# Transposing SwiGLU results by DMA in 16-bit halves instead of on TensorE

## The chip, the core and the metric

The kernel runs on one core of one Trainium2 chip. Its time is the device time of one execution in microseconds, here the median of three runs. The engines of the core are TensorE (PE in the profile; PEld is its weight load), VectorE (DVE), ScalarE (ACT), GpSimd (POOL) and SyncE (SP). SP and GpSimd issue the loads of the weights; sixteen DMA engines carry them out.

## What is computed

Two layers of a hybrid decoder on one sequence of 512 tokens with 1024 features, all in float32:

```python
for l in range(DEPTH):                      # DEPTH = 2
    x = x + 0.5 * swiglu(rms_norm(x, ffn1_norm[l]), ffn1_wg[l], ffn1_wu[l], ffn1_wd[l])
    h = rms_norm(x, mix_norm[l])
    z = h @ w_in[l]                         # q, k, v and three inputs of a short convolution
    ...                                     # sliding-window attention (128), gated convolution
    x = x + concat([attn_out, conv_out]) @ w_out[l]
    x = x + 0.5 * swiglu(rms_norm(x, ffn2_norm[l]), ffn2_wg[l], ffn2_wu[l], ffn2_wd[l])
return rms_norm(x, final_norm)

def swiglu(h, w_gate, w_up, w_down):        # 1024 -> 2816 -> 1024
    return (silu(h @ w_gate) * (h @ w_up)) @ w_down
```

So there are four SwiGLUs, which make up most of the work, and the change touches only these. The 2816 inner features are 22 blocks of 128, taken as 11 pairs of blocks.

## The kernel before

Every float32 product is made of three products of rounded parts: an operand is split into a high part (a cast on ScalarE, L213) and a low part (the difference, on VectorE, L214), and high x high, high x low and low x high are summed in PSUM. This holds for weights (`raw` to `wh` and `wl`, three buffers each) and for activations.

**Groups of seven.** The large products are done as 2 x 2 blocks with seven block products in place of eight. `Seven` (L567) makes the seven forms of the activation side: `b11`, `b21`, `t2`, `t3`, `t1`, `t4`, `b22`, each split into parts in 4 KB buffers (pool `xf`, 14 of them, function `form`). On the weight side the sums of blocks are made by accumulating DMAs on GpSimd's queue (L208, L279) and by additions on VectorE (L249). `CHAINS` gives the order of the seven steps. A step is two weight groups (h = 0 and 1) of twelve matmuls each.

**Stages.** Each SwiGLU is a list of stages. `p` is a plain pair, `w` a pair of inner blocks by seven steps (`winograd2`, L988), `u` the same in another form (`winograd`), `d` a plain down projection of one or two pairs, `s` a down projection of four pairs by seven steps (`share`, L817), and `e` the last one of the program (`Finale.last`). The lists are

```python
FIRST = (("p",0),("p",1),("d",(0,)),("w",2),("d",(1,)),("w",4),("w",6),("w",8),("u",10),("s",2),("d",(10,)),("s",6))
INNER = (("p",0),("d",(0,)),("w",1),("w",3),("w",5),("w",7),("w",9),("s",1),("s",5),("d",(9,10)))
LAST = INNER[:-2] + (("e", 5),)
```

The first SwiGLU uses `FIRST`, the second and third `INNER`, the fourth `LAST`. A stage `s` or `e` takes its activations from `raws`: two pairs make the four blocks of one group of seven. So in each SwiGLU four pairs feed groups of seven (`blocks`), sixteen in all. In the two `INNER` ones pair 9 goes into the plain down projection at the end (with the plain pair that is left over), and in `LAST` pair 9 is handled by `few`.

**The turn.** `winograd2` leaves its results `ups[0..3]` with tokens on the partitions (128 tokens x 512 features each). The down projection needs features on the partitions. `turn(c)` (L1045 on) transposes four 128 x 128 blocks on TensorE into PSUM (L1050), and ScalarE copies the 128 x 512 result to `raws` (L1057; L1054 for `few`), or `split` makes its parts (for pair 9 of `INNER`). The four turns of a pair are kept in `pending` and taken out by `flush`: one each after steps 0 and 1 and two after step 2 of the next stage (`turns`), or in a later `d` or `s` stage.

**Order.** The program is written in the order of the work; a planner gives every engine its own queue, in which instructions stand in the order of the program as far as their inputs and buffers are free at the planned time. `tc.issue_after(ins)` holds what is written in its block behind one given instruction of the same engine. Each queue then runs strictly in order. Weights are loaded four units ahead (`LOAD_AHEAD`) and split two groups ahead (`SPLIT_AHEAD`); SP issues a load (L196) when one of eight `raw` buffers is free.

**Other buffers.** `g2` has 14 buffers of 2 KB per partition (gates, results, evictions, and the eight partial results of `Apart` in the stages `s` of all but the first SwiGLU), `g8` four of 8 KB (`raws` and the scaled input of the norm).

Of the kernel before, what the change touches and what calls it, by code (L numbers as in the profile page):

```python
# [8 lines left out]
F32 = mybir.dt.float32  # L9
F32R = mybir.dt.float32r  # L10
BF16 = mybir.dt.bfloat16
I32 = mybir.dt.int32
AF = mybir.ActivationFunctionType
ALU = mybir.AluOpType

P = 128
D = 1024
S = 512
# [53 lines left out]
def trunk_kernel(  # L72
# [55 lines left out]
    def f32(ap):  # L128
        return ap.bitcast(F32)


    zero = const.tile([P, S], BF16, name="zero")
    nc.vector.memset(zero, 0.0)
# [76 lines left out]
            state["raw"] += 1  # L210

    def split(hi, lo, raw, eng=nc.vector):
        nc.scalar.copy(hi, raw)  # L213
        eng.tensor_sub(lo, raw, f32(hi))  # L214

    def split_far(hi, lo, raw):

# [4 lines left out]
    def need_split(g):  # L222
        while state["split"] <= min(g, len(order) - 1):
# [330 lines left out]
    class Seven:  # L554
# [8 lines left out]
        def make(self, *names):  # L563
            for what in names:
                if what in self.forms:
                    continue
                b11, b12, b21, b22 = (  # L567
                    self.full[j][:, :, t * H : (t + 1) * H] for j in range(2) for t in range(2)
                )
# [319 lines left out]
    def ffn(norm, stages, after=None, late=None):  # L889
# [102 lines left out]
        def winograd2(b, between=None):  # L992
# [47 lines left out]
                if between:  # L1040
                    between(step)
            if b in blocks:
                raws[b] = g8(f"raw_a_{name}", F32, (P, KC // 2, S))
            if b in few:
                raws[b] = [form(f"raw_a{n}_{name}", F32, (P, 2, S)) for n in range(2)]  # L1045

            def turn(c, tag="sc"):
# [5 lines left out]
                if b in few:  # L1053
                    nc.scalar.copy(raws[b][c // 2][:, c % 2, :], tp)  # L1054
                    return
                if b in raws:
                    nc.scalar.copy(raws[b][:, c, :], tp)  # L1057
# [5 lines left out]

            pending.extend(lambda *tag, c=c: turn(c, *tag) for c in range(NT))

        def shared(b):
            return Seven([raws[b], raws[b + 2]], room_form, f"s_{norm.i}_{b}")

        def turns(step):

            if step < 2:
                flush()
            if step == 2:
                flush(2, "mm")

        sevens = [b for what, b in stages if what == "s"]
        blocks = [b + j for what, b in stages if what in "se" for j in (0, 2)]
        few = [b + 4 for what, b in stages if what == "e"]
        raws = {}
        pending = []  # L1080

# [7 lines left out]
        for i, (what, b) in enumerate(stages):  # L1089
# [10 lines left out]
            if what == "s" and end:  # L1100
                ends = [
                    Seven(full, None, f"e_{n}")
                    for n, full in enumerate(([raws[b + 4], raws[b + 6]], raws[b + 8]))
                ]

                def between(step):
# [3 lines left out]
                        if step == at:  # L1110
                            ends[n].make(operand)

                share(ops, 0.5, between, apart)
            elif what == "e":
                end.last(ends)
                return
            elif what == "s" and b == sevens[0]:
# [1 line left out]
                share(  # L1119
                    ops,  # L1120
                    0.5,
                    ahead(then, {3: ("b11",), 4: ("b21",), 5: ("t2",), 6: ("t3",)}),
                    apart,
                )
            elif what == "s" and i + 1 == len(stages):
# [464 lines left out]
```

## Time and profile before

| | |
|---|---|
| median of three runs | 1678.69 us (1678.51 to 1679.63) |
| the profiled execution | 1678.83 us |
| its span, first to last instruction | 1677.0 us |
| granted TensorE clock, mean | 0.999 |
| TensorE matmul, busy | 1668.1 us (99%) |
| VectorE, busy | 1388.3 us (83%) |
| ScalarE, busy | 979.6 us (58%) |
| moved by DMA | 285.15 MB, mean 170 GB/s |

Times are of one profiled execution. A row of a group gives line, engine, operation, output and inputs by their names in the program, shapes and count, then the busy time of the group in us and the mean of one in ns, then idle time of the engine before them and what ended it. A row of a timeline gives start and length in us, both from the start of the span. Matmuls overlap, so that the distance from one start to the next, and not the length, is what one costs. A row of stretches gives the busy time of each engine with its number of instructions, the granted clock, the mean busy share of the sixteen DMA engines, and what they moved in GB/s.

### The profile page before, as it was taken

To read this page: it belongs to the slowest core of one execution; us is meant where nothing else is said; L and a number is where in the kernel's file an instruction comes from. 1 tells how busy PE (TensorE), PEld (TensorE's weight loads), DVE (VectorE), ACT (ScalarE), POOL (GpSimd) and SP (SyncE) were. 2 spreads that over 40 slices of the span, in tenths; PEclk is the share of its full clock that TensorE was granted. 3 is DMA by queue.
4 is the path that set the end of the run, shared out by engine and by line. 5 is a ranking of instruction groups with operands and counts; after the bars stand their busy time and mean duration, and the time that the engine had idled before them with its cause. 6 is when DMAs were issued, how large, how long until landed. Compare 5 with 4: busy or idle time off the path is not lost.

```text
span 1677.0 us, 22346 instructions
## 1 busy us (share of the span) xinstructions
PE 1668.1 (99%) x8396; PEld 1414.0 (84%) x8396; DVE 1388.3 (83%) x1824; ACT 979.6 (58%) x1361; POOL 211.2 (13%) x188
## 2 busy tenths in 40 slices
PE   9999999999999999999999999999999999999998
PEld 7888889988898888888888888888888988888886
DVE  7987679988899976799798677997788998667997
ACT  6445565466566655575465555654565766556655
POOL 0011111001211111111011111110012111111121
PEclk9999999999999999999999999999999999999999
DMA  8467777731497777778567777785125967777892
GB/s 252 99 177 189 188 195 186 188 98 51 113 228 175 177 187 185 183 197 204 173 139 179 187 187 188 189 209 167 51 64 130 233 140 194 185 187 179 224 252 74
DMA packets 192545, 285.15 MB, mean 170 GB/s; under 512 B 9068, under 2 KB 77748, under 8 KB 192436
## 3 DMA queue, kind: packets, MB, share of 16 engines
q1 hardware_dynamic: 151844, 201.26, 38.1%
q0 software_dynamic: 39872, 81.80, 28.6%
q8 instruction: 66, 1.08, 0.3%
q10 hardware_dynamic: 720, 0.66, 0.1%
q14 instruction: 43, 0.35, 0.1%
HBM read 262.71 MB, written 2.10 MB: 158 GB/s over the span
## 4 chain that ended last, share of the span: by engine, by line
PE 96%; issue 1%; DMA 1%; DVE 1%; ACT 0%; POOL 0%; SPq 0%; POOLq 0%; DVEq 0%; ACTq 0%
PE x L813 25%; PE y L813 12%; PE acc L308 8%; PE acc L309 8%; PE acc L311 7%; PE x_s L813 6%; PE w L813 6%; PE y_s L813 3%; PE x_s L798 3%; PE at L1050 2%; PE x_m L798 2%; PE w_s L813 2%; PE y_s L798 1%; PE x_e L813 1%; PE y_m L798 1%; PE acc L693 1%
## 5 line engine op out<-in xcount | busy, mean ns | idle before, releaser
L213 ACT CAST wh<-raw 128x1024 fp32r<-128x1024 f32 (+1 forms) x491 | 513.0, 1045 | 535.8 <-PE x L813 129.1
L214 DVE TENSOR_TENSOR wl<-raw,wh 128x1024 fp32r<-128x1024 f32 (+1 forms) x491 | 598.3, 1221 | 202.8 <-ACT wh L213 201.2
L308 PE MATMUL acc<-xh,wh 128*128 128x512 f32 x424 | 165.8, 392 | 0.0
L309 PE MATMUL acc<-xl,wh 128*128 128x512 f32 x424 | 165.5, 390 | 0.0
L311 PE MATMUL acc<-xh,wl 128*128 128x512 f32 x416 | 162.3, 390 | 0.0
L208 POOL DMA_DIRECT2D raw<-in_ffn_wu_dram x39 | 48.9, 1254 | 419.7 <-DMA raw<-in_ffn_wu_dram 340.2
L309 PEld LDWEIGHTS acc<-xl,wh 128*128 128x128 f32 x424 | 79.7, 188 | 15.9 <-DVE xl L489 0.2
L308 PEld LDWEIGHTS acc<-xh,wh 128*128 128x128 f32 x424 | 79.8, 188 | 15.6
L311 PEld LDWEIGHTS acc<-xh,wl 128*128 128x128 f32 x416 | 78.1, 188 | 16.4
L208 POOL DMA_DIRECT2D raw<-in_ffn_wg_dram x39 | 48.0, 1255 | 221.1 <-DMA raw<-in_ffn_wu_dram 84.1
L208 POOL DMA_DIRECT2D raw<-in_ffn_wd_dram x34 | 41.0, 1207 | 259.4 <-DMA raw<-in_ffn_wd_dram 112.0
L249 DVE TENSOR_TENSOR raw<-raw,raw 128x1024 f32<-128x1024 f32 x56 | 68.0, 1219 | 2.4 <-DMA raw<-in_ffn_wu_dram 1.7
L813 PE MATMUL w<-wh,fb21h 128*128 128x512 f32 x152 | 60.7, 399 | 0.0
L813 PE MATMUL x<-wh,ft2h 128*128 128x512 f32 x152 | 60.6, 398 | 0.0
L813 PE MATMUL y<-wh,ft3h 128*128 128x512 f32 x152 | 60.4, 398 | 0.0
L813 PE MATMUL w<-wl,fb21h 128*128 128x512 f32 x152 | 59.4, 391 | 0.0
L813 PE MATMUL x<-wl,ft2h 128*128 128x512 f32 x152 | 59.3, 390 | 0.0
L813 PE MATMUL y<-wh,ft3l 128*128 128x512 f32 x152 | 59.2, 390 | 0.0
L813 PE MATMUL y<-wl,ft3h 128*128 128x512 f32 x152 | 59.2, 390 | 0.0
L813 PE MATMUL w<-wh,fb21l 128*128 128x512 f32 x152 | 59.2, 389 | 0.0
L813 PE MATMUL x<-wl,fb11h 128*128 128x512 f32 x152 | 59.2, 389 | 0.0
L813 PE MATMUL x<-wh,ft1l 128*128 128x512 f32 x152 | 59.1, 389 | 0.0
(602 smaller groups left out, 4586.4 us busy)
## 6 DMA issues: line engine op xcount, KB each, us to landing
raw<-in_ffn_wu_dram SPq DMA_DIRECT2D x126, 512.0 KB, 4.4
raw<-in_ffn_wd_dram SPq DMA_DIRECT2D x105, 512.0 KB, 5.7
raw<-in_ffn_wg_dram SPq DMA_DIRECT2D x86, 512.0 KB, 4.7
raw<-in_ffn_wu_dram POOLq DMA_DIRECT2D x39, 512.0 KB, 8.1
raw<-in_ffn_wg_dram POOLq DMA_DIRECT2D x39, 512.0 KB, 6.2
raw<-in_w_in_dram SPq DMA_DIRECT2D x36, 512.0 KB, 3.6
raw<-in_ffn_wd_dram POOLq DMA_DIRECT2D x34, 512.0 KB, 9.0
raw<-raw POOLq DMA_DIRECT2D x21, 512.0 KB, 8.3
```

The costliest lines, as they stand in the source:

```text
L208: nc.gpsimd.dma_start(out=r, in_=rows_of(*more), accum_op=ALU.add)
L213: nc.scalar.copy(hi, raw)
L214: eng.tensor_sub(lo, raw, f32(hi))
L249: nc.vector.tensor_add(a11, a11, s1)
L308: nc.tensor.matmul(acc, hi[:, k, :], rhs[k][0], start=k == first, stop=False)
L309: nc.tensor.matmul(acc, hi[:, k, :], rhs[k][1], start=False, stop=False)
L311: nc.tensor.matmul(acc, lo[:, k, :], rhs[k][0], start=False, stop=k == last)
L693: nc.tensor.matmul(opening[n], (lo if part == "w" else hi)[:, k, :], xl if part == "x" else xh, start=n not in begun, stop=k == KC - 1 and ...
L798: nc.tensor.matmul(accs[c // 2][:, c % 2, :], w[:, k, cols], x_[:, 2 * h + k, :], start=start and c % 2 == 0 and h + k + i == 0, stop=h + ...
L813: nc.tensor.matmul(accs[u], x_[:, 2 * h + k, tok], w[:, k, :], start=start and h + k + i == 0, stop=h + k == 2 and i == 2, skip_group_chec ...
L1050: nc.tensor.transpose(tp[:, t * P : (t + 1) * P], ups[t][:, c * P : (c + 1) * P], ident)
```

## The change

The turns on TensorE go away for the sixteen pairs that feed groups of seven and for pair 9 of the two `INNER` SwiGLUs. The four turns of `few` in `LAST` stay. In their place each result of 128 x 512 float32 words is looked at as 1024 halves of 16 bits. ScalarE copies it so that all the low halves lie together and all the high halves lie together (`lay_apart`); SP issues DMA transposes of 16-bit elements from one SBUF tile to another; and ScalarE puts the transposed halves together into words again (`join`).

For a pair of a group of seven (`Crossing`) two of the four results are laid apart and sent after step 0 of the next stage and two after step 1, one DMA of 256 KB each. Two of the four columns are joined after step 5 and two after step 6; for the last of the four pairs all four are joined after step 3 of the stage `s` (`joined`). For pair 9 (`Tail`) the same goes on inside the first stage `s`: laid and sent after steps 1 and 2, with two DMAs of 128 KB for each result, joined after steps 5 and 6, and split in the second stage `s`. The joins stand behind the last weight cast written before them. `Seven` takes its blocks through a function, since they are not there yet when it is made.

```diff
+    def words(ap):
+        return ap.bitcast(U16).rearrange("p (n two) -> p two n", two=2)
+
+    def lay_apart(src, name):
+        halves = g2(f"halves_{name}", U16, (P, 2, S))
+        nc.scalar.copy(halves, words(src))
+        return halves
...
     def split(hi, lo, raw, eng=nc.vector):
-        nc.scalar.copy(hi, raw)
+        cast = nc.scalar.copy(hi, raw)
         eng.tensor_sub(lo, raw, f32(hi))
+        return cast
...
-                split(hi, lo, raw)
+                state["cast"] = split(hi, lo, raw).ins
...
             if b in blocks:
-                raws[b] = g8(f"raw_a_{name}", F32, (P, KC // 2, S))
+                crossing.append(Crossing(b, name, ups))
+                return
+            if b in tails:
+                crossing.append(Tail(b, name, ups))
+                return
...
-                if b in raws:
-                    nc.scalar.copy(raws[b][:, c, :], tp)
-                    return
...
+        class Crossing:
...
+            def step(self):
+                n = self.steps
+                self.steps += 1
+                if n == 0:
+                    self.to = g8(f"turned_{self.name}", U16, (P, 2, NT, S))
+                for t in {0: (0, 1), 1: (2, 3)}.get(n, ()):
+                    halves = lay_apart(self.ups[t], f"{self.name}_{t}")
+                    nc.sync.dma_start_transpose(
+                        self.to.rearrange("p a c s -> p (a c) s")[:, :, t * P : (t + 1) * P],
+                        halves.rearrange("p a n -> p (a n)"),
+                    )
+                if n in (5, 6) and self.b != max(blocks):
+                    self.join(*((0, 1), (2, 3))[n - 5])
+                    return n == 6
+                return False
+
+            def join(self, *cs):
+                if self.b not in raws:
+                    raws[self.b] = g8(f"raw_a_{self.name}", F32, (P, KC // 2, S))
+                with tc.issue_after(state["cast"]):
+                    for c in cs:
+                        nc.scalar.copy(words(raws[self.b][:, c, :]), self.to[:, :, c, :])
+
+        class Tail:
...
+            def during(self, n):
+                if n == 1:
+                    self.to = [form(f"turned{h}_{self.name}", U16, (P, NT, S)) for h in range(2)]
+                for t in {1: (0, 1), 2: (2, 3)}.get(n, ()):
+                    halves = lay_apart(self.ups[t], f"{self.name}_{t}")
+                    for h in range(2):
+                        nc.sync.dma_start_transpose(
+                            self.to[h][:, :, t * P : (t + 1) * P], halves[:, h, :]
+                        )
+                if n == 5:
+                    self.whole = g8(f"raw_a_{self.name}", F32, (P, 2, 2, S))
+                if n > 4:
+                    whole = self.whole[:, n - 5].rearrange("p c s -> p (c s)")
+                    with tc.issue_after(state["cast"]):
+                        for h in range(2):
+                            nc.scalar.copy(
+                                words(whole)[:, h, :],
+                                self.to[h][:, 2 * (n - 5) : 2 * (n - 4), :].rearrange("p c s -> p (c s)"),
+                            )
+
+            def parts(self, j):
+                hi, lo = acts[self.b + j] = [form(f"a{n}_{self.name}_{j}", shape=(P, 2, S)) for n in "hl"]
+                split(hi, lo, self.whole[:, j])
...
+        def joined(between):
+            def step(n):
+                if n == 3:
+                    crossing.pop(0).join(0, 1, 2, 3)
+                if crossing and isinstance(crossing[-1], Tail):
+                    crossing[-1].during(n)
+                between(n)
+            return step
...
         def turns(step):
...
+            crossing[:] = [c for c in crossing if not c.step()]
...
             elif what == "s":
                 def between(step):
-                    if 2 <= step < 6:
-                        flush(1, "aux")
+                    if step in (2, 4):
+                        crossing[0].parts(step // 2 - 1)
```

More of the change, by code (lines that the diff above doesn't have):

```diff
@@ L11 @@
 BF16 = mybir.dt.bfloat16
+U16 = mybir.dt.uint16
 I32 = mybir.dt.int32
@@ L566, in make @@
                     continue
+                full = self.full() if callable(self.full) else self.full
                 b11, b12, b21, b22 = (
-                    self.full[j][:, :, t * H : (t + 1) * H] for j in range(2) for t in range(2)
+                    full[j][:, :, t * H : (t + 1) * H] for j in range(2) for t in range(2)
                 )
@@ L1064, in winograd2, with __init__ @@
             pending.extend(lambda *tag, c=c: turn(c, *tag) for c in range(NT))
-        def shared(b):
-            return Seven([raws[b], raws[b + 2]], room_form, f"s_{norm.i}_{b}")
+        class Crossing:
+            def __init__(self, b, name, ups):
+                self.b, self.name, self.ups = b, name, ups
+                self.steps = 0
+                self.to = None
+            def step(self):
[19 more added lines that the diff above has]
+                        nc.scalar.copy(words(raws[self.b][:, c, :]), self.to[:, :, c, :])
@@ new lines, in ffn, with __init__, step @@
+        class Tail:
+            def __init__(self, b, name, ups):
+                self.b, self.name, self.ups = b, name, ups
+            def step(self):
+                return False
+            def during(self, n):
[20 more added lines that the diff above has]
+                split(hi, lo, self.whole[:, j])
@@ L1074, in turns @@
                 flush(2, "mm")
+            crossing[:] = [c for c in crossing if not c.step()]
+        crossing = []
         sevens = [b for what, b in stages if what == "s"]
@@ L1078, in ffn @@
         few = [b + 4 for what, b in stages if what == "e"]
+        tails = [b[0] for what, b in stages if what == "d" and len(b) == 2]
         raws = {}
@@ L1102, in ffn @@
                     Seven(full, None, f"e_{n}")
-                    for n, full in enumerate(([raws[b + 4], raws[b + 6]], raws[b + 8]))
+                    for n, full in enumerate((lambda b=b: [raws[b + 4], raws[b + 6]], raws[b + 8]))
                 ]
@@ L1111, in between @@
                             ends[n].make(operand)
-                share(ops, 0.5, between, apart)
+                share(ops, 0.5, joined(between), apart)
             elif what == "e":
@@ L1121, in ffn @@
                     0.5,
-                    ahead(then, {3: ("b11",), 4: ("b21",), 5: ("t2",), 6: ("t3",)}),
+                    joined(ahead(then, {3: ("b11",), 4: ("b21",), 5: ("t2",), 6: ("t3",)})),
                     apart,
```

1 line of the change is left out of this document (added).

## The prediction

> **What bounds the kernel now.** I read the busy shares first, then the chain that ended last, then the groups of ScalarE, then the stages one by one. The page's busy shares and its chain:
>
> ```profile
> span 1677.0 us, 22346 instructions
> PE 1668.1 (99%) x8396; PEld 1414.0 (84%) x8396; DVE 1388.3 (83%) x1824; ACT 979.6 (58%) x1361; POOL 211.2 (13%) x188
> ...
> PE 96%; issue 1%; DMA 1%; DVE 1%; ACT 0%; POOL 0%; SPq 0%; POOLq 0%; DVEq 0%; ACTq 0%
> PE x L813 25%; PE y L813 12%; PE acc L308 8%; PE acc L309 8%; PE acc L311 7%; PE x_s L813 6%; PE w L813 6%; PE y_s L813 3%; PE x_s L798 3%; PE at L1050 2%; PE x_m L798 2%; PE w_s L813 2%; PE y_s L798 1%; PE x_e L813 1%; PE y_m L798 1%; PE acc L693 1%
> ```
>
> TensorE is the bound: 96% of the chain is its work, and 2% is line 1050, the transposes that the change takes away. The sum is made against this profiled execution: 1678.83 us, of which the span is 1677.0 and 1.8 lies around it; the median of the three runs, 1678.69, is 0.14 lower, so nothing has to be converted. A difference of 0.2% (3.4 us) is about what a measurement of this kernel can tell from none.
>
> **What is removed from TensorE.** The groups of ScalarE count the turns, since each turn is four transposes and one reading of the result:
>
> ```profile
> L213 ACT CAST wh<-raw 128x1024 fp32r<-128x1024 f32 (+1 forms) x491 | 513.0, 1045 | 535.8 <-PE x L813 129.1 <-issue 93.4 <-PE y L813 84.2
> L1057 ACT COPY raw_a<-at 128x512 f32<-128x512 f32 x64 | 35.8, 586 | 3.1 <-PE at L1050 3.0
> ...
> L1003 ACT COPY p<-x 128x512 f32<-128x512 f32 x38 | 22.2, 585 | 12.0 <-PE x L813 12.0
> ...
> L213 ACT CAST ah<-at 128x512 fp32r<-128x512 f32 x8 | 4.6, 580 | 0.0
> ...
> L1054 ACT COPY raw_a<-at 128x512 f32<-128x512 f32 x4 | 2.1, 586 | 0.0
> ```
>
> 64 turns feed the sixteen pairs of the groups of seven, 8 the two inner last pairs, 4 the last pair of the final SwiGLU. The first 72 go; the 4 of line 1054 stay. What one turn costs the chain is read where it cuts into a row of matmuls (TensorE's timeline; start, duration):
>
> ```profile
> 919.20 0.39 PE L813 MATMUL x<-wh,fb11l 128*128 128x512 f32 x1
> 919.43 0.39 PE L813 MATMUL x<-wl,fb11h 128*128 128x512 f32 x1
> 919.66 0.38 PE L1050 MATMUL at<-ident,u 128*128 128x128 f32 x2
> 919.88 0.38 PE L1050 MATMUL at<-ident,p 128*128 128x128 f32 x2
> 920.01 0.48 PE L813 MATMUL w<-wh,fb21h 128*128 128x512 f32 x1
> 920.33 0.40 PE L813 MATMUL w<-wh,fb21l 128*128 128x512 f32 x1
> 920.56 0.40 PE L813 MATMUL w<-wl,fb21h 128*128 128x512 f32 x1
> ```
>
> A matmul follows the one before by 0.227 us. Without the turn the two matmuls after it would start at 919.66 and 919.89; the second starts at 920.33, so this turn costs 0.44 us, not the 4 x 0.27 that the durations suggest (they overlap). Over a whole pair's stage, from the chain in order of time (two steps at its start, the same place one stage later, and steps between):
>
> ```profile
> 948.86 10.88 PE x L813 x48
> ...
> 960.18 5.50 PE w L813 x24
> ...
> 966.12 5.46 PE x L813 x24
> ...
> 972.45 5.46 PE y L813 x24
> ...
> 988.79 10.88 PE x L813 x48
> ```
>
> The stage is 988.79 - 948.86 = 39.93 us with four turns, and seven steps of 10.88 / 2 = 5.44 would be 38.1: 1.85, or 0.46 a turn, the slower matmuls behind it included. I take that: 72 x 0.46 = 33.1 us. (The page's 2% of 1677 is 33.5 for 76 turns, 0.44 each, 31.7 for 72.)
>
> **What is added to ScalarE.** Per pair, four copies that lay the halves apart and four that join them go in, each of 1024 halves per partition; four copies of 0.586 go out. No row shows a 16-bit copy. The lower end is 0.586 (512 words, as if the halves went two at a time), the upper twice the 128x1024 cast, 2.09; I take the cast's 1.045, which has the same number of elements. Per pair +8 x 1.045 - 4 x 0.586 = +6.0 us, 96 us over sixteen pairs; per tail +8 x 1.045 + 2 x 1.045 - 4 x 0.580 = +8.1, 16 over two. ScalarE goes from 980 to some 1092 of 1646 us. Whether that is hidden is decided by stage. A pair's stage, the last pair's (with the operands for the next group), an inner first group of seven, and the second:
>
> ```profile
> 659.60:699.70 40.10, 40.10 (x187) 33.28 (x186) 27.95 (x29) 22.08 (x29) 5.40 (x5) 1.00 0.74 183
> 699.70:739.70 40.00, 40.00 (x186) 33.22 (x185) 36.61 (x37) 27.71 (x35) 3.76 (x4) 1.00 0.73 184
> 739.70:777.80 38.10, 38.10 (x170) 31.56 (x169) 37.08 (x37) 25.91 (x30) 6.44 (x6) 1.00 0.87 216
> 777.80:820.00 42.20, 42.20 (x207) 35.26 (x206) 33.83 (x40) 18.58 (x21) 4.20 (x4) 1.00 0.75 192
> ```
>
> (The columns are length, then busy TensorE, weight loads, VectorE, ScalarE, GpSimd, then clock, DMA share, GB/s.) An ordinary pair's stage comes to 22.1 + 6.0 = 28.1 of 38.1 us: it fits. Within it the first step has two casts, two evictions and two lays, 2 x 1.045 + 2 x 0.585 + 2 x 1.045 = 5.35 of a step's 5.44: full, but not over, and the casts have slack:
>
> ```profile
> 940.51 1.05 ACT L213 CAST wh<-raw 128x1024 fp32r<-128x1024 f32 x1 [1.19 <-PE x L813]
> 943.23 1.05 ACT L213 CAST wh<-raw 128x1024 fp32r<-128x1024 f32 x1 [1.67 <-PE x L813]
> ...
> 941.60 1.22 DVE L214 TENSOR_TENSOR wl<-raw,wh 128x1024 fp32r<-128x1024 f32 x1 [1.49 <-ACT wh L213]
> ```
>
> The cast starts when TensorE frees one of three buffers; groups come 2.72 apart, so this one is wanted 2 x 2.72 later, at 945.95, and VectorE has it at 942.82. Slack 3.1 us. Behind a late cast on ScalarE queue the next evictions, and VectorE's difference and then TensorE wait for it. Two lays (2.1) fit into 3.1.
>
> The inner first group of seven is another matter: it gets four lays and four joins of the tail and the four joins of the previous pair, 12 x 1.045 = 12.5, and 25.9 + 12.5 = 38.4 of 38.1 us: over-full, while VectorE is busy for 37.1 of it. The join of four at its step 3 holds the next cast for 4.2 us, of which the slack takes 3.1, and what the next group's operands (b21, t2) need from that pair now comes after step 3 instead of well before. I price it at 1.1 for that join and 2.1 for one pair of copies without room, some 3 us in each of the two stages, 6 in all, between 0 (the cast ahead takes the slack) and 12.5 each, 25 in all (nothing hidden). The two other stages that take a join of four have no tail: 25.9 + 4.2 = 30.1 of 38 if they are like this one, so nothing. VectorE's change is small: four differences of a tail, x8 in all,
>
> ```profile
> L214 DVE TENSOR_TENSOR al<-at,ah x8: 683/684/684, 796.2 to 1149.2; 128x512 fp32r<-128x512 f32 x8
> ```
>
> become two of 1.22: 2.7 against 2.4 us.
>
> **What is added to the DMA and to SP's queue.** Four transposes of 256 KB per pair, eight of 128 KB per tail: 64 + 16 instructions on SP, 18.9 MB. No transpose is in the trace. The nearest rows are the queues in a stretch of the mixer, where rows of 512 bytes are loaded, and in a pair's stage (919 to 957):
>
> ```profile
> q1 hardware_dynamic: 6512, 3.67, 20.2%
> ...
> q1 hardware_dynamic: 2720, 5.24, 44.0%
> q0 software_dynamic: 1287, 2.50, 39.8%
> ```
>
> In the first 0.202 x 16 x 60 us / 6512 = 30 ns a packet of 563 bytes; in the second 98 ns for 1926 bytes; the accumulating loads take 188 ns. By bytes (5.24 MB in 0.44 x 38 us, 313 GB/s) a transpose is 0.84 us of all 16 engines. If it moves as 1024 rows of 128 halves, 64 to an engine, it is 1.9 us at 30 ns, 6.3 at 98 and 12 at 188. Ends 0.84 and 12; I take 1.9, the packet nearest in size. A pair's stage has 0.26 x 40.1 = 10.4 us of DMA left, or 2.6 per transpose; four of 1.9 make 7.7. It is hidden, with little over: DMA at (29.7 + 7.7) / 38.1 = 98%. If that cover goes, each further microsecond per transpose costs 4 us a stage, 64 in all. The transposes themselves have time: laid in steps 0 and 1, joined in 5 and 6, some 20 us later.
>
> The Trainium skill, "DMA: Bandwidth & Descriptors", section "Latency and other measured facts", gives 261 GB/s for a DMA transpose; by it one would be 1.0 us (an estimate) and the sum the same. "VectorE: DVE Perf Modes", section "The three transpose paths", speaks against the change: 1309 ns for a 128x128 block against 390 on TensorE; eight such blocks one after another would be 10.5 us (an estimate), and the first rival below would hold. No row of this trace decides between them.
>
> SP is in order, so a transpose that waits for ScalarE holds the weight loads behind it. What SP does now:
>
> ```profile
> SPq L196 <- DVE wl L214: 1072.1, 298, 22.3
> ...
> 962.61 2.90 SPq L196 DMA_DIRECT2D raw<-in_ffn_wu_dram  x2
> 967.82 3.59 SPq L196 DMA_DIRECT2D raw<-in_ffn_wg_dram  x2
> ...
> raw<-in_ffn_wu_dram SPq DMA_DIRECT2D x6, 512.0 KB, 4.1
> ```
>
> It mostly waits for raw buffers. In the stage that starts at 948.86 + 5.44 = 954.3 the first loads go out at 962.6 and land by about 970; they serve step 5, which starts at 972.45 + 2 x 5.44 = 983.3 and whose cast comes 5.44 earlier, near 978: 8 us of slack, against one step (5.4 us) that a transpose may have to wait for its lay. The accumulating loads on GpSimd's queue are moved past nothing. Cost nothing, up to 2 us a pair (32) if the slack is used twice. Buffers: counted from the code, the 2 KB, 8 KB and 4 KB pools reach 12 of 14, 4 of 4 and 14 of 14 with the new tiles, so each just fits.
>
> **Sum.** 1678.8 - 33.1 + 6 = 1652 us.
>
> **Rivals.** First, *the transposes fill the DMA engines*: the weights come late and TensorE waits in each pair's stage. For it: 74% busy there already, and an unknown price whose ends straddle 2.6 us, the point from which it decides. Against: 188 GB/s is far from the 313 that the loads reach. At 4 us a stage needs 29.7 + 16 = 45.7 us of DMA against 38.1 of TensorE, +7.6 x 16 = +122: 1646 + 122 = 1768 us. At 6.3 it is 54.9, +269, 1915; at 12, 77.7, +634, 2280. This is the case of the skill's 1309 ns.
>
> Second, *ScalarE becomes the bound*, because a copy with a stride of two halves takes 2.09 us: a pair's stage comes to 22.1 - 2.3 + 16.7 = 36.5 of 38.1, still inside; a first group of seven with a tail to 25.9 + 25.1 = 51 of 38.1, +13 twice; the other two joins of four hold a cast 8.4 - 3.1 = 5.3, twice; and the first steps, 2.1 + 1.2 + 4.2 = 7.5 against 5.44, use 2 of the 3.1 twice running, about 1 us a pair, 16. 1646 + 26 + 11 + 16 = 1699 at the worst, about 1680 with half of it caught up. Against it: elements, not bytes, set the rows of 512 and 1024.
>
> Third, *the turns were hidden*, VectorE being the bound beside them: 1678. VectorE is at 92 to 97% from 700 to 778 us; but no turn lies in most of that stretch, and elsewhere it is at 70%. At most the 2 x 8 turns next to it, 7 us, would be lost.
>
> **Chances.** Forecast 0.52 (own range 1644 to 1671, from stalls of 0 to 25 us). DMA bound 0.36, of which most above 1690. ScalarE 0.09, half within 0.2%. Turns hidden 0.03. Faster 0.54, same 0.05, slower 0.41. The low end is 1644 (no stall, and a turn at the 0.48 that 966.12 - 960.18 - 5.44 = 0.50 allows now and then); the high end must take in nearly half of the first rival, up to its 1768.
>
> **What would show it.** Right: only the last SwiGLU's four turns left (16 transposes), ScalarE near 1090 us, 16-bit copies near 1.05, pairs' stages of 38.1 us, DMA share there under 1, TensorE's idle time under 10 us and mostly in the two inner first groups of seven. Wrong: casts or additions of weights whose releaser is a DMA, transposes that land 10 us or more after issue, stages over 40 us.

## The result and the profile after

The changed kernel takes 1657.43 us in the median of four runs (1656.70 to 1658.67) against 1678.61 for the kernel before: the ratio is 0.9873, with a 95% interval from 0.9856 to 0.9890. It is faster by 21 us, where 26.6 were forecast. The profiled execution has a span of 1656.1 us. The busy shares, the chain by engine, and SP's queue from its page:

```profile
PE 1639.9 (99%) x8108; PEld 1385.0 (84%) x8108; DVE 1381.2 (83%) x1820; ACT 1091.6 (66%) x1437; POOL 212.3 (13%) x188
...
q1 hardware_dynamic: 228132, 220.14, 45.4%
...
PE 92%; DVE 4%; ACT 2%; issue 1%; DMA 0%; SPq 0%; DVEq 0%; ACTq 0%
```

There are 288 matmuls fewer. TensorE has 92% of the chain and no longer 96: 4% are now VectorE and 2% ScalarE, work that TensorE waited for. Line numbers have moved: L813 of before is L825, L213 and L214 are L223 and L224, L249 is L260.

The new instructions: joins and lays among the groups of ScalarE, then the transposes from the view of the tile they write and read (SP's time to issue one, shortest, median, longest; and issue to landing), then SP's queue in one pair's stage from 905.6 to 943.7 us (packets, MB, share):

```profile
L1112 ACT COPY raw_a<-turned 128x1024 uint16<-128x1024 uint16 x64 | 83.8, 1357 | 0.0
L138 ACT COPY halves<-p 128x1024 uint16<-128x1024 uint16 x36 | 37.2, 1038 | 0.0
L138 ACT COPY halves<-u 128x1024 uint16<-128x1024 uint16 x36 | 36.0, 1047 | 0.0
```

```profile
L1096 SPq DMA_TRANSPOSE turned<-halves x64: 1237/1238/3412, 122.6 to 1526.5; - x64
L1131 SPq DMA_TRANSPOSE turned<-halves x16: 1195/1680/2570, 737.4 to 1084.8; - x16
...
DMA to landing us min/median/max: 2.7/5.0/8.8
```

```profile
q1 hardware_dynamic: 6948, 6.30, 59.2%
```

A lay takes 1.04 us, a join 1.36. Against the same stage before (2720 packets, 44.0%) SP's queue moves 4228 packets more, four transposes of 1024 and a few, in 0.592 x 16 x 38.1 - 0.440 x 16 x 38 = 93 us of engine time: 22 ns a packet. 64 packets on each engine make a transpose of 256 KB 1.4 to 1.5 us of all sixteen.

Where the gain stayed and where it didn't is seen by laying the same place of the program side by side. In the chain in order of time, two places of the kernel before, of the changed one, and of the first experiment below, which has the turns taken away and nothing added:

```profile
150.00 10.88 PE x L813 x48
...
468.37 5.75 PE x_m L798 x48
...
694.41 10.88 PE x L813 x48
...
908.94 10.88 PE x L813 x48
```

```profile
147.47 10.88 PE x L825 x48
...
465.54 5.75 PE x_m L810 x48
...
686.11 10.88 PE x L825 x48
...
900.18 10.88 PE x L825 x48
...
938.26 10.88 PE x L825 x48
```

```profile
147.26 10.88 PE x L813 x48
...
460.17 5.75 PE x_m L798 x48
...
680.67 10.88 PE x L813 x48
...
891.46 10.88 PE x L813 x48
```

From the first pair of rows of each: the first SwiGLU from its third step-wise pair on (pairs 6 and 8, u10, both groups of seven), with the mixer behind it up to its output product, took 318.4, 318.1 and 312.9 us. From the second pair: the last inner pair of the second SwiGLU with both groups of seven, to the pairs of the third, 214.5, 214.1 and 210.8. The other places are read in the same way, each column from one profiled execution:

| part of the span, us | before | changed | no turns | lost by what is added |
|---|---|---|---|---|
| first SwiGLU from its third step-wise pair, to the mixer's output product | 318.4 | 318.1 | 312.9 | 5.2 |
| second SwiGLU's last pair and groups of seven | 214.5 | 214.1 | 210.8 | 3.3 |
| third SwiGLU's, with the mixer behind | 303.1 | 302.1 | 299.0 | 3.1 |
| fourth SwiGLU's, to the end | 150.2 | 150.1 | 148.5 | 1.6 |
| all else | 690.8 | 671.8 | 671.5 | 0.3 |
| span | 1677.0 | 1656.1 | 1642.6 | 13.5 |

In ordinary pairs' stages everything expected was gained: 938.26 - 900.18 = 38.08 us, seven steps of 5.44 without a gap. All but 0.3 us of the loss lies in the four parts where a SwiGLU passes from its pairs to its groups of seven. About 1.5 of the first part's 5.2 belong to this one execution: two of the runs below, in which nothing of the first SwiGLU's lays is changed and TensorE waits there just as long, take 316.6 us for it (with the tails on TensorE, and with the join in two pieces), a loss of 3.7. The reason is shown below, with the stage u10. The medians of all runs give 12.6 us for the whole loss, where these two executions give 13.5.

The stretches of the second SwiGLU in the changed kernel (pair 7's stage; pair 9's, with one step ahead of it; first group of seven; second group, with 4 us of the stage behind it; columns as before):

```profile
648.00:686.10 38.10, 38.10 (x170) 31.56 (x169) 27.73 (x29) 28.13 (x33) 4.85 (x4) 1.00 0.93 221
686.10:729.60 43.50, 43.50 (x194) 36.03 (x193) 40.79 (x43) 33.69 (x40) 4.83 (x4) 1.00 0.89 216
729.60:770.00 40.40, 40.00 (x176) 32.49 (x175) 31.98 (x32) 35.59 (x39) 6.62 (x6) 1.00 1.00 223
770.00:815.00 45.00, 44.02 (x206) 35.44 (x205) 41.54 (x47) 22.36 (x23) 4.17 (x4) 1.00 0.80 208
```

In the first group ScalarE is busy for 35.6 of 40.4 us, and VectorE's work has moved: 32.0 us there (37.1 before) and 41.5 of 45 in the last stretch, of which 38.2 fall into the 41 us of the second group itself (33.8 of 42 before). DMA is at 100% in the first group too, so that this view alone doesn't say which of the two is the cause. The chain that ended last goes through ScalarE's copies in the first group, and through VectorE's work left over from it in the second:

```profile
747.30 1.88 ACT halves L138 x2
...
752.21 3.77 ACT raw_a L1112 x3
...
773.32 2.35 DVE wl L224 x2
```

ScalarE's timeline in the first group, and VectorE's at the same time:

```profile
750.04 1.35 ACT L1112 COPY raw_a<-turned 128x1024 uint16<-128x1024 uint16 x1
751.25 1.07 ACT L877 ACTIVATE apart<-y_s 128x512 f32<-128x512 f32 x2
752.21 3.77 ACT L1112 COPY raw_a<-turned 128x1024 uint16<-128x1024 uint16 x3
755.83 2.00 ACT L223 CAST wh<-raw 128x1024 fp32r<-128x1024 f32 x2
```

```profile
750.17 1.23 DVE L224 TENSOR_TENSOR wl<-raw,wh 128x1024 fp32r<-128x1024 f32 x1 [2.10 <-ACT wh L223]
755.58 0.69 DVE L880 SCALAR_TENSOR_TENSOR apart<-x_s,apart 128x512 f32<-128x512 f32 x1 [4.18 <-PE x_s L825]
756.91 1.23 DVE L224 TENSOR_TENSOR wl<-raw,wh 128x1024 fp32r<-128x1024 f32 x1 [0.64 <-ACT wh L223]
```

With the evictions among it the join of four holds the weight casts for 5.8 us, and VectorE stands still for 4.2 of them, in a stretch where it had one microsecond to spare (37.1 of 38.1 before). By the row it stands for an eviction of TensorE's running product, which is next in its queue; the low part behind that waits 0.64 us more for its cast.

### The profile page after: what moved, and what is told of

Read it like the earlier page. It is cut to its first block, busy times and chain, and to the rows that moved or that the text cites. A ratio compares the mean times of both kernels' runs of the same rounds, so it can differ in the third digit from the quotient of the medians.

```text
span 1656.1 us, 22077 instructions
## 1 busy us (share of the span) xinstructions
PE 1639.9 (99%) x8108; PEld 1385.0 (84%) x8108; DVE 1381.2 (83%) x1820; ACT 1091.6 (66%) x1437; POOL 212.3 (13%) x188
## 4 chain that ended last, share of the span: by engine, by line
PE 92%; DVE 4%; ACT 2%; issue 1%; DMA 0%; SPq 0%; DVEq 0%; ACTq 0%
PE x L825 25%; PE y L825 12%; PE acc L319 8%; PE acc L320 8%; PE acc L322 8%; PE w L825 6%; PE x_s L825 5%; PE x_m L810 3%; PE x_s L810 2%; PE y_s L825 2%; DVE wl L224 2%; PE y_s L810 1%; PE y_m L810 1%; PE x_e L825 1%; PE w_s L825 1%
## 5 line engine op out<-in xcount | busy, mean ns | idle before, releaser
L223 ACT CAST wh<-raw 128x1024 fp32r<-128x1024 f32 (+1 forms) x491 | 512.1, 1045 | 401.5 <-PE x L825 94.0
L224 DVE TENSOR_TENSOR wl<-raw,wh 128x1024 fp32r<-128x1024 f32 (+1 forms) x491 | 595.5, 1220 | 164.8 <-ACT wh L223 164.2
L1112 ACT COPY raw_a<-turned 128x1024 uint16<-128x1024 uint16 x64 | 83.8, 1357 | 0.0
L260 DVE TENSOR_TENSOR raw<-raw,raw 128x1024 f32<-128x1024 f32 x56 | 67.9, 1222 | 1.1 <-DMA raw<-in_ffn_wu_dram 0.5
L825 PE MATMUL w<-wh,fb21h 128*128 128x512 f32 x152 | 59.2, 390 | 0.0
L825 PE MATMUL x<-wh,ft2h 128*128 128x512 f32 x152 | 59.2, 390 | 0.0
L825 PE MATMUL y<-wh,ft3h 128*128 128x512 f32 x152 | 59.2, 390 | 0.0
L825 PE MATMUL x<-wl,ft1h 128*128 128x512 f32 x152 | 59.2, 389 | 0.0
L825 PE MATMUL x<-wh,ft1h 128*128 128x512 f32 x152 | 59.1, 389 | 0.0
L825 PE MATMUL w<-wl,fb21h 128*128 128x512 f32 x152 | 59.1, 389 | 0.0
L825 PE MATMUL x<-wl,ft2h 128*128 128x512 f32 x152 | 59.1, 389 | 0.0
L825 PE MATMUL w<-wh,fb21l 128*128 128x512 f32 x152 | 59.1, 389 | 0.0
L825 PE MATMUL x<-wh,ft2l 128*128 128x512 f32 x152 | 59.1, 389 | 0.0
```

The costliest lines, as they stand in the source:

```text
L223: cast = nc.scalar.copy(hi, raw)
L260: nc.vector.tensor_add(a11, a11, s1)
L825: nc.tensor.matmul(accs[u], x_[:, 2 * h + k, tok], w[:, k, :], start=start and h + k + i == 0, stop=h + k == 2 and i == 2, skip_group_chec ...
L1112: nc.scalar.copy(words(raws[self.b][:, c, :]), self.to[:, :, c, :])
```

## The experiments

All ran beside the kernel before, which took 1678.5 to 1678.8 us each time.

**The turns alone.** The kernel before, with the transposes taken out:

```diff
-                tp = psum(tag, [P, S], f"at_{name}_{c}")
-                for t in range(NT):
-                    nc.tensor.transpose(...)
+                if b in few:
+                    ...                         # as before
+                else:
+                    tp = ups[c]
```

> The kernel before, with the 288 transposes of the 72 turns left out: ScalarE and the split read the result in SBUF as it lies, so tokens and features stay unturned and the output is not the reference's. Nothing is added on ScalarE, SP or the DMA. Theory A (TensorE is the bound everywhere, the change pays 12 us for what it adds): 1678.7 - 33.1 = 1646 us. Theory B (part of the turns was hidden, because VectorE had to be waited for in stage u10 and the groups of seven behind it): the 1.75 us of u10 and part of the 2 x 1.85 of the tails stay, 1648 to 1651, and TensorE shows waits for VectorE without any new work.

Measured 1644.83 us, ratio 0.9802 (0.9788 to 0.9817). That is 33.7 us less than before, 0.47 for each of 72 turns: theory A. None of the turns was hidden. This kernel leaves the turning out and serves for its time alone. What the change adds costs 1657.4 - 1644.8 = 12.6 us.

**The join of four earlier.**

```diff
-                if n == 3:
+                if n == 1:
                     crossing.pop(0).join(0, 1, 2, 3)
```

> The changed kernel with the join of four of the last pair after step 1 of the first group of seven instead of after step 3. Theory A (the late join holds back b21 and t2 of the next group, so VectorE's work for them moves into the second group, where it is full): most of the 12 us comes back, 1648 to 1653. Theory C (ScalarE is simply full in the first group, wherever the joins stand): 1656 to 1662, since steps 1 and 2 also hold the tail's lays.

Measured 1665.61 us, 0.9926 (0.9911 to 0.9941): slower than the change by 8, and worse than either theory had it. Its waits show where:

```profile
PE w_s L825 <- DVE wl L224: 11.0, 2, 5.7
...
DVE raw L260 <- DMA raw<-in_ffn_wd_dram: 10.6, 4, 3.2
```

TensorE waits 11.0 us in two places, the second and the third SwiGLU's groups of seven, for a weight's low part that stands on VectorE behind an addition of weights whose load is late. The order of all queues is planned anew when one instruction moves, so this run doesn't show that the late join is harmless; it shows that the place of the join can cost more than it brings.

**The tails back on TensorE.** The turns stand in the second group of seven, as before.

```diff
-        tails = [b[0] for what, b in stages if what == "d" and len(b) == 2]
+        tails = []
...
-                    if step in (2, 4):
-                        crossing[0].parts(step // 2 - 1)
+                    if 2 <= step < 6:
+                        flush(1, "aux")
```

> The changed kernel with pair 9 of the two inner SwiGLUs turned on TensorE as before; the sixteen other pairs stay on the DMA. TensorE gets back 8 turns, 3.7 us. Theory A (the join of four is what stalls, the tail's copies cost nothing): 1657.4 + 3.7 = 1661. Theory C (ScalarE is over-full because of the tail's 8 copies in the first group): the stalls of the two inner groups, 3.2 + 2.7 us, go, and 1657.4 + 3.7 - 5.9 = 1655.

Measured 1658.81 us, 0.9882 (0.9867 to 0.9896), between the two numbers, and not to be told from the change. In the second SwiGLU's part of the table it takes 213.9 us against 214.1: the four turns back in cost 1.85, and the stall falls from 3.3 to 1.3. Moving the tails to the DMA brought nothing on balance. The 1.3 that are left go when the join of four is taken in two pieces as well, as a run below shows.

**Each transpose of the pairs twice.**

```diff
+                    spare = g2(f"spare_{self.name}_{t}", U16, (P, 2 * NT, P))
+                    nc.sync.dma_start_transpose(spare, halves.rearrange("p a n -> p (a n)"))
```

> The changed kernel with each transpose of the sixteen pairs issued a second time into a spare tile that nothing reads: 64 more of 256 KB. The trace of the changed kernel puts one at 64 packets of 24 ns, 1.5 us of all engines. If DMA shares add up as the prediction had it (free 10.4 us a stage, threshold 2.6 us per transpose), two of 1.5 are 3.0 each, 1.6 us a stage too much, 1657 + 16 x 1.6 = 1683. If the share of busy time overstates what is needed, it costs nothing but SP's issue time, 1657 to 1660.

Measured 1704.09 us, 1.0150 (1.0133 to 1.0167): 47 us more, where adding up shares gave 26. The waits:

```profile
DVE raw L260 <- DMA raw<-in_ffn_wu_dram: 51.5, 14, 6.6
...
PE x L825 <- DVE wl L224: 15.8, 10, 3.5
```

The weights that are summed by accumulating loads come late, in fourteen places, and VectorE stands in front of their addition with the next weight's low part behind it. That fits the margin that the prediction saw (2.6 us per transpose of 256 KB), since two transposes of 1.5 are past it. But the second transposes also take 64 x 1.2 us of SP's time, ahead of loads, and in the chain of a pair's stage their issuing stands just ahead of a late load. This run doesn't part the two, so the margin of the DMA engines is not shown.

**ScalarE's copies without the DMA, and the DMA without the copies.** Both have the tails on TensorE, and each leaves a part of the turning out. The first writes the halves straight into the tile that the transposes filled; the second transposes the result as it lies, makes no use of what it transposed, and in place of a join copies 512 unturned words.

```diff
-                    halves = lay_apart(self.ups[t], f"{self.name}_{t}")
-                    nc.sync.dma_start_transpose(...)
+                    nc.scalar.copy(self.to[:, :, t, :], words(self.ups[t]))
```

```diff
-                    halves = lay_apart(self.ups[t], f"{self.name}_{t}")
                     nc.sync.dma_start_transpose(
                         ...
-                        halves.rearrange("p a n -> p (a n)"),
+                        self.ups[t].bitcast(U16),
                     )
...
-                        nc.scalar.copy(words(raws[self.b][:, c, :]), self.to[:, :, c, :])
+                        nc.scalar.copy(raws[self.b][:, c, :], self.ups[c])
```

> The kernel with the two tails on TensorE, and for the sixteen pairs ScalarE's copies without the DMA: the lay writes its halves straight into the tile that the transposes filled, so nothing is turned and the output is not the reference's. With neither copies nor transposes it would be 1644.8 + 3.7 (8 turns of the tails) = 1648.5 us, with both it was 1658.8. Theory S (ScalarE's copies cause the 10 us, by delaying the casts in stage u10 and in the first groups of seven): 1656 to 1659. Theory D (the transposes cause it, by delaying weights on SP's queue and the DMA engines): 1648 to 1651.

> The counterpart: tails on TensorE, the 64 transposes of the pairs as they are but taken from the result itself, with nothing laid apart; the join is a copy of 512 words of the unturned result (0.585 us, as many as the kernel before had). What is turned is not used, and the output is not the reference's. Theory S: 1648 to 1651 us. Theory D: 1656 to 1659. Both in part: the two surcharges over 1648.5 add up to about the 10 us.

Measured 1657.82 us (0.9874, 0.9859 to 0.9889) for the copies alone and 1650.37 (0.9831, 0.9816 to 0.9846) for the transposes alone. Over the 1648.5 that were worked out for neither, the copies cost 9.3 us and the transposes 1.9; with both it is 10.3. Theory S. In the profiled executions most of the 1.9 can't be the transposes': 1.4 us lie ahead of the first of them, since the first large product starts at 17.0 us here and at 15.6 in the kernel without turns. The first three rows of the table, by the same marks, take what they take without turns, plus 1.85 for the four turns of each tail. With the copies alone TensorE waits where it waits in the change (the first row, in the first SwiGLU, is one of the two such waits); with the transposes alone no wait for a cast or a weight's low part is left. The second row stands for the input at the start, and only one wait, also at the start, is longer:

```profile
PE y_s L810 <- ACT wh L223: 1.3, 1, 1.3
```

```profile
PE xt L671 <- DMA xin<-in_x_dram: 1.1, 1, 1.1
```

**Stage u10 spread.** In the first SwiGLU the last pair's lays go one to a step:

```diff
-                for t in {0: (0, 1), 1: (2, 3)}.get(n, ()):
+                for t in ({n: (n,)} if first and self.b == max(blocks) else {0: (0, 1), 1: (2, 3)}).get(n, ()) if n < NT else ():
```

> The changed kernel, but in the first SwiGLU the results of the last pair are laid apart and sent one per step over the four first steps of stage u10, not two per step. A step there is 2.88 us, not 5.44, and two lays (2.1) and a cast (1.05) and two evictions (0.74) don't fit into it. If that is the 4 to 5 us lost between u10 and the second group of seven: 1652 to 1654. If the join of four in that group loses it: 1657.

Measured 1657.39 us, 0.9871 (0.9857 to 0.9886): no difference in the time. In the profile, the first SwiGLU's part takes 315.6 us, 1.0 less than the 316.6 of undisturbed executions without the spread, and the first of TensorE's two waits there falls from 1.0 to 0.2 us; the second, 1.3, stays. The fourth part, whose code is that of the change, took some 1.6 longer in this execution. So spreading the lays mends a quarter of what is lost at u10 at most, too little to be told from such differences.

**The same with the tails on TensorE and the join of four in two pieces.**

```diff
-                if n == 3:
-                    crossing.pop(0).join(0, 1, 2, 3)
+                if n == 2:
+                    crossing[0].join(0, 1)
+                if n == 3:
+                    crossing.pop(0).join(2, 3)
```

> Tails on TensorE, u10 spread as in the kernel beside it, and the join of four split into two after step 2 and two after step 3. Both mends work: 1658.8 - 4 - 3 (half of the 1.5 in each of three groups, and the rest of the first) = 1652. Only the spread works: 1654 to 1655. If splitting the join brings what the join after step 1 brought (weights late in the group behind it): 1660 or more.

Measured 1653.94 us, 0.9853 (0.9837 to 0.9870): 4.9 less than with the tails on TensorE alone. By the marks of the table 0.8 of it lies in the first SwiGLU's part, where the spread acts, and 1.2 to 1.3 in each of the others, where only the join changed. The second SwiGLU's part is now 212.7, which is the 210.8 without turns and the tail's 1.85: no stall is left there, and 0.4 in the fourth. 2.9 us stay lost in the first.

**The join in two pieces alone**, with the edit just above as the only one of the changed kernel, tails by DMA:

> The changed kernel with only the join of four split into two after step 2 and two after step 3; tails and stage u10 as in the change. If the 5.05 us that the four copies hold ScalarE in one piece is what starves the casts: 1652 to 1654. If the tail's eight copies in the same group keep ScalarE full (35.6 of 40.4 us): 1655 to 1658.

Measured 1656.94 us, 0.9866 (0.9853 to 0.9880). It mends the fourth SwiGLU (148.8 of 150.1), which has no tail, and hardly the second (213.5) and third (301.8): there the tail's copies keep ScalarE busy for 35.3 of 40 us. It takes both, the join in pieces and the tail away: one takes 0.6 off the stall of the second, the other 2.0, both together all 3.3.

**The tails later.** Spread and two pieces, with the tail's lays after steps 4 and 5 of the first group, its joins after 2 and 3 of the second, its splits after 4 and 5.

```diff
-                for t in {1: (0, 1), 2: (2, 3)}.get(n, ()):
+                for t in {4: (0, 1), 5: (2, 3)}.get(n, ()):
...                                             # the tail's joins become a method of their own
-                    if step in (2, 4):
-                        crossing[0].parts(step // 2 - 1)
+                    if step in (2, 3):
+                        crossing[0].join(step - 2)
+                    if step in (4, 5):
+                        crossing[0].parts(step - 4)
```

> Stage u10 spread, join of four split, and the tails by DMA after all, but later: laid and sent after steps 4 and 5 of the first group, joined after steps 2 and 3 of the second, where ScalarE was busy for 18.6 of 42 us before the change, split after steps 4 and 5. If it fits there: the 8 turns are saved, 1653.9 - 3.7 = 1650. If the copies only move the stall: 1654 to 1658.

Measured 1661.91 us, 0.9898 (0.9884 to 0.9912): a miss on the far side of both numbers. The chain in the second group shows a load of weights in it:

```profile
778.13 9.12 DMA raw<-in_ffn_wd_dram
```

The eight DMAs of the tail now stand on SP's queue between 755 and 772 us, just ahead of loads that this group wants. Whether SP's order or the DMA engines make that load late was not tried.

**The ordinary joins earlier**, after steps 3 and 4 (on top of the kernel with tails on TensorE, spread, two pieces):

```diff
-                if n in (5, 6) and self.b != max(blocks):
-                    self.join(*((0, 1), (2, 3))[n - 5])
-                    return n == 6
+                if n in (3, 4) and self.b != max(blocks):
+                    self.join(*((0, 1), (2, 3))[n - 3])
+                    return n == 4
```

> Tails on TensorE, u10 spread, join of four split (1653.9 us), and now the ordinary joins after steps 3 and 4 instead of 5 and 6, so that in the first SwiGLU the four joins of the third pair (5.4 us in one row just ahead of u10) are done before the silus of step 6. If these are what delays b21 and the casts of u10: 2 to 3 us less, 1651 to 1652. If u10 and the group behind it are full anyway (VectorE was busy for 60.7 of 62.2 us there before the change): 1654.

Measured 1652.51 us, 0.9842 (0.9828 to 0.9855): 1.4 less, between the two numbers. The profiles don't put that gain where the joins are: the first SwiGLU's part is 0.3 shorter, the three others are the same to 0.02, and the first large product simply starts 1.9 us earlier (16.1 against 18.0), ahead of any join; the stage of the second step-wise pair is 0.7 longer, with a wait for a transpose in the chain. Here ScalarE waits for transposes, 14.9 us in twelve places, up to 2.4: two steps after the last lay is about as early as a join can stand, and it isn't shown that earlier joins bring anything.

**The first SwiGLU's last pair back on TensorE**, with the tails there too and the join of four in two pieces:

```diff
-            if b in blocks:
+            if b in blocks and first and b == max(blocks):
+                raws[b] = g8(f"raw_a_{name}", F32, (P, KC // 2, S))
+            elif b in blocks:
                 crossing.append(Crossing(b, name, ups))
...                                             # turn(c) copies to raws again, as before the change
```

> Tails on TensorE and the join of four split, and in the first SwiGLU the last pair back on TensorE too (four turns in u10, 1.85 us). If its lays in u10 and its joins behind it are the 2.9 us still lost there: 1653.9 + 1.85 - 2.9 = 1653. If it is the joins of the pair before, or VectorE: 1655 to 1656.

Measured 1651.07 us, 0.9833 (0.9819 to 0.9846), the fastest of those that leave nothing out. It is 2.9 faster than the kernel with tails on TensorE, spread and two pieces (1653.94), which has that pair on the DMA. Not all of this is the pair's: by the profiles the first large product starts 1.3 earlier and the fourth part is 0.4 shorter. The first SwiGLU's part goes from 315.8 to 314.7, with four turns more on TensorE: that one pair on the DMA cost 1.1 + 1.85 = 2.9 there with its lays spread, and 3.7 without. 314.7 is the 312.9 without turns and 1.85: nothing is lost there any more. Why, the stretches of u10 and of the group behind it show, before and after the change:

```profile
235.30:257.20 21.90, 21.90 (x187) 21.90 (x186) 20.86 (x25) 15.47 (x25) 3.24 (x4) 1.00 0.74 174
257.20:297.50 40.30, 40.30 (x337) 40.30 (x337) 39.80 (x43) 23.49 (x26) 4.96 (x5) 1.00 0.80 196
```

```profile
229.10:249.20 20.10, 20.10 (x169) 20.05 (x168) 16.30 (x20) 17.40 (x25) 2.39 (x2) 1.00 0.96 188
249.20:294.70 45.50, 42.71 (x339) 42.10 (x338) 41.72 (x45) 27.67 (x30) 6.61 (x6) 0.96 0.71 186
```

Before, VectorE was busy for 60.7 of 62.2 us in the two. Afterwards it gets 4.6 us less done in u10, which is 1.8 us shorter and in which it waits for ScalarE, whose load there rises from 15.5 of 21.9 to 17.4 of 20.1. What is left over delays the next group: in ScalarE's queue a cast of activations waits 4.5 us for a result of VectorE (L608) and holds the weight casts behind it, for which TensorE waits twice:

```profile
PE y_s L810 <- ACT wh L223: 1.3, 1, 1.3
PE x_s L810 <- ACT wh L223: 1.0, 1, 1.0
```

The clock of 0.96 in the second stretch is the other part of the loss in this execution. Behind the second wait TensorE's matmuls start 0.21 us apart for 3 us, and then 0.12 again; the granted clock from 264 to 269 us is 0.66. The chain shows it as 44 matmuls in 6.65 us, against 48 in 5.76 before:

```profile
264.69 6.65 PE x_s L810 x44
```

```profile
268.71 5.76 PE x_s L798 x48
```

The two executions with 316.6 us have the same two waits and a clock of 1.00 behind them, so the lower clock doesn't follow every such wait.

## The prediction against the runs

- **The turns.** 72 x 0.46 = 33.1 us; measured 33.7. Right, and the third rival (turns hidden) is out.
- **A lay and a join.** 1.045 for each; lays took 1.04, joins 1.36. The join writes with a stride of two halves, the lay reads with one. That elements and not bytes set the time of a copy couldn't be read from the rows of 512 and 1024 words, since both double; the lays show it, 1024 halves in the time of 1024 words. ScalarE's total of 1092 us came out, but by chance: the 72 joins alone are 72 x 0.31 = 22 us above the price, and the busy time, which counts overlapping instructions once, hides them.
- **Pairs' stages: hidden.** Right to 0.3 us over all else than the four parts of the table: ScalarE 28.1 of 38.1 us, as worked out (with the same luck on the joins).
- **The transposes.** 1.9 us of the DMA engines taken, 1.5 measured; the pairs' stages run at a DMA share of 0.93 (98% was expected). Hidden: at most 1.9 us in the run that has them alone, most of it ahead of the first transpose. The first rival, with 0.36 of the chances, didn't happen, but the run with double transposes shows that there is little room: one of 1.5 is hidden, a second one costs 47 us, in the engines or on SP's queue. Of the two figures of the Trainium skill, "DMA: Bandwidth & Descriptors" ("Latency and other measured facts", 261 GB/s) is nearer: 256 KB in 1.5 us are 175 GB/s. Eight times the 1309 ns of the Trainium skill, "VectorE: DVE Perf Modes" ("The three transpose paths") would be 10.5 us, an estimate, and even from issue to landing, weights loading beside it, the median is 5.0.
- **SP's queue.** The prediction let a transpose wait one step (5.4 us) for its lay. SP stood at one for up to 19.7 (in all, times, longest):

```profile
SPq L1096 <- ACT halves L138: 245.5, 32, 19.7
```

  That cost nothing in the pairs' stages, as the table shows.
- **The stall.** This is the term that was mis-sized: 6 us in all, 3 in each inner first group of seven, and nothing in the two other stages with a join of four. The inner two lost 3.3 and 3.1, as priced, and for the reasons given: without the tail's copies 1.3 are left of each, where the join was priced at 1.1 beyond the slack. The other two lost 5.2 (3.7 at the full clock) and 1.6. The prediction carried the inner stage's row over to them ("25.9 + 4.2 = 30.1 of 38 if they are like this one") and counted ScalarE's free time alone, though it priced the same join at 1.1 beyond the slack in the inner stage. The first SwiGLU's isn't like it: u10's steps are 2.88 us long, VectorE was full in u10 and behind it, and a lay or a join that delays a cast there has no slack on the engine behind. In the fourth, the join of four takes 5.0 us in one piece; VectorE waits 2.3 of them for what is joined, and TensorE later 1.8 for an eviction that VectorE has late (0.2 before, the last row):

```profile
DVE raw_a L591 <- ACT raw_a L1112: 2.3, 1, 2.3
PE x_e L825 <- DVE bias L1305: 1.8, 1, 1.8
```

```profile
PE x_e L813 <- DVE bias L1206: 0.2, 1, 0.2
```

- **The signs.** TensorE's idle time was to be under 10 us and mostly in the two inner first groups. It is 1656.1 - 1639.9 = 16.2 us, against 8.9 before, and the largest part that the change adds, 2.8, is in the first SwiGLU.
- **The forecast** of 1652 us (own range 1644 to 1671) against 1657.4: the mechanism held, the stall was 12.6 us instead of 6. The range is wider than the gain of 21 us, so that lying in it says little; the terms say more.

## What to carry to other kernels

When work moves from a full engine to one that is 60% busy, look at the stretches where the engine that waits for it is also full: the mean of the receiving engine says nothing there, and here the gain was lost in those few places alone. Copies that stand ahead of others' inputs are better cut into pieces shorter than the slack of what queues behind them (here 3.1 us; two joins fit, four don't). And a conversion needn't be done everywhere: leaving 12 of 72 turns on TensorE (and splitting the join of four) took 6 us off the changed kernel. When two runs differ by a microsecond or two, lay their parts side by side before naming a cause: some of it can lie where nothing was changed.

## What the runs showed of the hardware

A ScalarE copy of 1024 16-bit elements per partition takes 1.04 us when it reads with a stride of two and 1.36 when it writes with one. A DMA transpose of 256 KB from SBUF to SBUF takes SP 1.24 us to issue and moves as packets of 256 bytes at about 22 ns each, against the 30 ns of packets of 563 bytes in the mixer; all 80 of them, 16 of which have 128 KB, landed within 2.7 to 8.8 us of their issue, half of them within 5.0. A turn of four float32 transposes costs TensorE 0.47 us amid matmuls. After two waits of 1.0 and 1.3 us the granted clock fell to 0.66 over 5 us in one execution, and in two others it didn't.
